# Expert weights in 2 MB slots of one piece, with the last expert's rows turned before the down product of the one before

## The chip, the cores and the metric

One core of a Trainium2 chip runs the kernel; the other cores are idle. The metric is the device time of one execution in microseconds (us). The engines' names here: PE or TensorE multiplies matrices and transposes (its weight loads are listed as PEld), DVE or VectorE and ACT or ScalarE work element by element, POOL or GpSimd too and issues some DMAs, SP or SyncE issues the DMAs of the weights. MB in the profile's rates are 10^6 bytes; a slot of 1 MB or 2 MB has 2^20 or 2^21 bytes.

## The reference

Two mixing blocks of sequence length 256 and width 1024 are computed first; the change lies in the mixture of experts behind them. It has 32 experts of width 1024, four of them for each token, all in fp32:

```python
def run_block(args):
    toks, e = args
    xb = h_pad[toks]
    gu = xb @ w_gu[e] + b_gu[e]
    g, u = gu[:, :D_EXPERT], gu[:, D_EXPERT:]
    g = jnp.minimum(g, SWIGLU_LIMIT)
    u = jnp.clip(u, -SWIGLU_LIMIT, SWIGLU_LIMIT)
    act = (u + 1.0) * (g * jax.nn.sigmoid(SWIGLU_ALPHA * g))
    return act @ w_dn[e] + b_dn[e]
```

The rows are weighted with the router's gates and summed for each token, and x + g_f times that sum is the output. h is modulated before: a normalised x times (1 + sc_f) plus sh_f.

## The kernel before

The two blocks run in the first 660 us or so; what follows is a loop over the 32 experts. Each expert has room for 64 of the 256 tokens (CAP); a loop over all experts for fuller ones stands behind a branch that this input doesn't take.

**The work of one expert.** For four experts at a time (GE) the rows are gathered: `gather` multiplies xh and xl (the two parts of the split x, tokens on the partitions) by the one-hot S, for each of 8 pieces k of 128 columns four matmuls of 256 columns, and `modulated` writes the piece of xg with a scale and a bias from mcol (k odd on ACT, L1280, k even on DVE, L1282). `up_proj` multiplies xg by w_gu into two PSUM tiles, G and U: for each k two halves hf of 512 columns for G and two for U, each with 64 of TensorE's columns, so that the two halves of a pair take their places side by side (L1310). `act` makes u from G and U on DVE and ACT (L1319 to L1325). `down_proj` turns u with four transposes T (L1334), ScalarE copies them to aT (L1336), and 32 matmuls make Y from aT and w_dn (L1344); a bias product stands ahead (L1339). DVE scales Y to y (L1347). `rows_T` transposes the gates GS to gst (L1298), and `combine` adds gst by y to four PSUM tiles acc (L1354).

**Weights.** `Ring` (L1181 to L1209) holds tiles e that SyncE fills in the order of their use: 8 slots for k of 1 MB (EARLY) that are loaded while the second block still runs, 10 more (LATE) and one on the tile h once they come free. A slot takes 128 rows of w_gu, 2048 values a row, or 256 rows of w_dn, two rows on a partition; it has 8 KB a partition. Slots 7 and 8 of LATE are two half tiles each (HALVES), with a DMA apiece. An expert needs 8 slots for up and 4 for down. A load waits until the products of the slot's last user are done.

**Order.** The loop for expert e writes: act, rows_T, up product k = 0 of e + 1, down product, combine, gathers for the next group (3, 3 and 2 of the k for the first three experts of a group), up product k = 1 to 7 of e + 1. For e = 30, up product k = 1 to 7 of expert 31 stands ahead of the down product. A scheduler orders each engine's instructions by what is ready, so what the code writes in one place can fill waits in another.

**Split weights.** In the blocks before the experts, `wchunk` splits each weight tile w into wh and wl (L200 and L201), from a rotation of NSPLIT = 6 each.

## Time and profile before

| what | value |
|---|---|
| runs | 1614.72, 1626.3, 1627.21 us; median 1626.3 |
| profiled execution | 1623.24 us |
| its span | 1621.5 us |
| granted clock of TensorE, mean | 0.983 |
| busy: PE | 1500.5 us, 93% |
| busy: PEld | 795.1 us, 49% |
| busy: DVE | 618.2 us, 38% |
| busy: ACT | 418.6 us, 26% |
| busy: POOL | 145.7 us, 9% |
| DMA | 518.96 MB, mean 320 GB/s |

The profile is of one execution. PE's rows count two records for each fp32 matmul; the order below counts one. The busy time of PE covers stages with different limits, and in the chain that ended last PE has 83%, DVE 9%, ACT 4%. "Idle before" is the time in which the engine stood still just ahead of a row, with what ended it behind the arrow.

### The profile page before, as it was taken

What the parts mean: (1) busy time and instruction counts of PE and PEld (TensorE: products, weight loads), DVE (VectorE), ACT (ScalarE), POOL (GpSimd) and SP (SyncE); (2) the same over time, 40 slices, a digit from 0 to 9 for tenths busy, and PEclk for the clock granted to TensorE, in tenths of its full rate; (3) what the DMA queues carried; (4) which work ended last, traced back from release to release, by engine and by line L of the source; (5) the groups of instructions that cost most, each with busy time, mean ns of one, the idle gap of its engine ahead of it and who ended that gap; (6) DMA issues with size and microseconds to landing.
All of it is one profiled execution on the core that took longest, in us unless ns stands there. A gap on an engine that the chain in (4) does not pass through costs nothing.

```text
span 1621.5 us, 19463 instructions
## 1 busy us (share of the span) xinstructions
PE 1500.5 (93%) x7533; PEld 795.1 (49%) x7533; DVE 618.2 (38%) x1337; ACT 418.6 (26%) x823; POOL 145.7 (9%) x210
## 2 busy tenths in 40 slices
PE   7999999998999999999899889889998998998997
PEld 5776778677767787533333333333333333333332
DVE  7666855687787875311111111111111111111111
ACT  4455455554566564200000000000000000000000
POOL 6640100010000000100000000000000000000000
PEclk9999999999999999999999999999999999999998
DMA  9464664464554358899999999999999999999993
GB/s 336 155 222 146 186 216 145 168 221 154 176 171 149 129 191 350 325 419 418 420 419 418 419 418 418 419 419 419 418 419 419 419 419 419 419 419 418 419 418 150
DMA packets 119316, 518.96 MB, mean 320 GB/s; under 512 B 13222, under 2 KB 22690, under 8 KB 75188
## 3 DMA queue, kind: packets, MB, share of 16 engines
q1 hardware_dynamic: 114288, 507.42, 79.8%
...
q8 instruction: 61, 1.00, 0.2%
...
q14 instruction: 35, 0.29, 0.0%
...
## 4 chain that ended last, share of the span: by engine, by line
PE 83%; DVE 9%; ACT 4%; issue 2%; DMA 1%; ACTq 0%; POOL 0%; SPq 0%; DVEq 0%
PE Y L1344 15%; PE G L1310 13%; PE U L1310 12%; PE pj L216 5%; PE pj L218 5%; PE pj L217 5%; PE acc L1354 4%; PE pj L235 2%; PE pj L236 2%; PE pm L1290 2%; PE pj L237 2%; PE T L1334 1%; PE pj L395 1%; DVE u L1325 1%; PE pj L226 1%
## 5 line engine op out<-in xcount | busy, mean ns | idle before, releaser
L1310 PE MATMUL G<-e,xg 128*64 128x512 f32 x1024 | 293.4, 596 | 2.2 <-DVE xg L1282 1.3
L1310 PE MATMUL U<-e,xg 128*64 128x512 f32 x1024 | 291.4, 594 | 0.0
L1344 PE MATMUL Y<-e,aT 128*64 128x512 f32 x1024 | 245.4, 620 | 1.7 <-ACT aT L1336 1.7
L116 DVE TENSOR_TENSOR wl<-w,wh 128x1024 fp32r<-128x1024 f32 (+2 forms) x155 | 185.9, 1209 | 66.8 <-ACT wh L115 65.7
L1321 ACT ACTIVATE s<-g 128x512 f32<-128x512 f32 x32 | 20.2, 630 | 653.3 <-DVE g L1319 653.3
L115 ACT CAST wh<-w 128x1024 fp32r<-128x1024 f32 (+2 forms) x155 | 156.2, 1013 | 85.4 <-PE pj L218 47.2
L1319 DVE TENSOR_SCALAR g<-G 128x512 f32<-128x512 f32 x32 | 22.1, 691 | 349.4 <-PE G L1314 349.4
L1310 PEld LDWEIGHTS U<-e,xg 128*64 128x64 f32 x1024 | 82.7, 137 | 145.5 <-issue 144.2
L1310 PEld LDWEIGHTS G<-e,xg 128*64 128x64 f32 x1024 | 79.6, 137 | 140.5 <-issue 129.7
L216 PE MATMUL pj<-wh,hTh 128*128 128x512 f32 (+4 forms) x352 | 131.0, 373 | 1.2 <-ACT hTh L115 1.0
L1344 PEld LDWEIGHTS Y<-e,aT 128*64 128x64 f32 x1024 | 69.2, 141 | 125.0 <-issue 114.8
L218 PE MATMUL pj<-wh,hTl 128*128 128x512 f32 (+4 forms) x352 | 129.0, 367 | 0.9 <-DVE hTl L116 0.9
L217 PE MATMUL pj<-wl,hTh 128*128 128x512 f32 (+4 forms) x352 | 129.3, 367 | 0.0
L1272 POOL TENSOR_SCALAR GS<-cst,posm,gate 128x128 f32<-128x128 f32 x64 | 51.1, 807 | 805.2 <-PE gst L1298 805.1
L1347 DVE TENSOR_TENSOR y<-Y,gfb 128x512 f32<-128x512 f32 x32 | 22.1, 691 | 232.3 <-PE Y L1344 232.3
L235 PE MATMUL pj<-hTh,wh 128*128 128x256 f32 x320 | 93.7, 293 | 0.2 <-DVE acc L926 0.2
L236 PE MATMUL pj<-hTl,wh 128*128 128x256 f32 x320 | 92.4, 289 | 0.0
L237 PE MATMUL pj<-hTh,wl 128*128 128x256 f32 x320 | 91.6, 288 | 0.1
L1354 PE MATMUL acc<-y,gst 64*128 64x512 f32 x256 | 63.6, 615 | 20.8 <-DVE y L1347 20.6
L216 PEld LDWEIGHTS pj<-wh,hTh 128*128 128x128 f32 x352 | 68.3, 194 | 19.5 <-issue 4.6
L218 PEld LDWEIGHTS pj<-wh,hTl 128*128 128x128 f32 x352 | 68.5, 195 | 12.9 <-DVE hTl L116 2.0
L217 PEld LDWEIGHTS pj<-wl,hTh 128*128 128x128 f32 x352 | 68.8, 196 | 9.6 <-issue 0.9
...
## 6 DMA issues: line engine op xcount, KB each, us to landing
e<-in_w_gu_dram SPq DMA_DIRECT2D x229, 1024.0 KB, 17.4
e<-in_w_dn_dram SPq DMA_DIRECT2D x115, 1024.0 KB, 17.4
...
```

The lines of the kernel that those rows point to most:

```text
L115: nc.scalar.copy(hi, src)
L116: nc.vector.tensor_sub(lo, src, hi.bitcast(F32))
L216: mm(ps[t][:, :n], X.hi[:, k, ts], wh[:, a:a + n], start=(k == 0), stop=False)
L217: mm(ps[t][:, :n], X.hi[:, k, ts], wl[:, a:a + n], start=False, stop=False)
L218: mm(ps[t][:, :n], X.lo[:, k, ts], wh[:, a:a + n], start=False, stop=(k == nk - 1))
L235: mm(p, wh[:, a:a + 128], X.hi[:, k], start=(k == 0), stop=False)
L236: mm(p, wh[:, a:a + 128], X.lo[:, k], start=False, stop=False)
L237: mm(p, wl[:, a:a + 128], X.hi[:, k], start=False, stop=(k == nk - 1))
L1272: nc.gpsimd.tensor_scalar(GS[:, t], slots[:, None, :].to_broadcast([128, 2, CAP]), posm[:, t, e:e + 1], gate[:, t, e:e + 1], op0=OP.is_equ ...
L1310: mm(P[64 * hf:64 * hf + 64, :], xk(k), w(c), start=(k == 0), stop=False)
L1344: mm(Y[64 * hf:64 * hf + 64, :], aT[:, 2 * (i % 2) + j, i // 2, :], w(D * j + 512 * hf), start=False, stop=(i == 3 and j == 1))
L1354: mm(acc[t][hf], gst[hs, t * 128:(t + 1) * 128], y[hs, :], start=False, stop=stop, **kw)
```

## The change

The ring's slots have 2 MB, 16 KB a partition in one piece, with one DMA each: 4 in EARLY and 5 in LATE, 18 MB in place of 19, without half tiles and without the slot on h. An up slot takes 256 rows of w_gu, with rows 2p and 2p + 1 on partition p, so a slot serves k = 0 and 1 (then 2 and 3, and so on); a down slot takes 512 rows of w_dn, four on a partition. An expert needs 4 slots for up and 2 for down. To match, `gather` reads xh and xl with a stride of two values, scale and bias of `modulated` come from a second tile mpair that is made like mcol (two DMAs on POOL's queue, two transposes, a copy), and T reads u with a stride of four values, where it was two.

`wh` and `wl` get explicit tags, so that the six pairs lie pair by pair. `act`, `turned` (the transposes and the copy) and `down_proj` are now three functions. For e = 30 the order is: T and aT of expert 30, up product k = 1 to 7 of expert 31, act and T of expert 31 (with s and aT in a free xg tile, `spare`), and then the down product of expert 30; for e = 31 only rows_T, the down product and combine are left.

The order of TensorE's instructions at two places, and SyncE's. First TensorE in the third expert of a group, from the second bias product of Y to gst. Before:

```order
L1339 MATMUL Y<-biases,selb 64x512
L1290 MATMUL pm<-S,xh 128x256
L1291 MATMUL pm<-S,xl 128x256
L1344 MATMUL Y<-e,aT 64x512 x4
L1290 MATMUL pm<-S,xh 128x256
L1291 MATMUL pm<-S,xl 128x256
L1290 MATMUL pm<-S,xh 128x256
L1291 MATMUL pm<-S,xl 128x256
L1290 MATMUL pm<-S,xh 128x256
L1291 MATMUL pm<-S,xl 128x256
L1344 MATMUL Y<-e,aT 64x512 x4
L1298 MATMUL gst<-cst,GS 128x128 x2
```

Now, from the same place:

```order
L1324 MATMUL G<-e,xg 64x512
L1302 MATMUL pm<-S,xh 128x256
L1302 MATMUL pm<-S,xl 128x256
L1302 MATMUL pm<-S,xh 128x256
L1302 MATMUL pm<-S,xl 128x256
L1324 MATMUL G<-e,xg 64x512
L1324 MATMUL U<-e,xg 64x512
L1302 MATMUL pm<-S,xh 128x256
L1302 MATMUL pm<-S,xl 128x256
L1302 MATMUL pm<-S,xh 128x256
L1302 MATMUL pm<-S,xl 128x256
L1324 MATMUL U<-e,xg 64x512
```

G and U here are halves of the pairs for k = 1 of the next expert. Behind the last row stand gst and then all 16 products of Y in one row: Y went from three pieces with gathers between them to the end, and one pair of G and one of U came in halves between the gathers.

The experts that gather nothing have the two whole pairs of k = 1 between the bias products and gst. At the end of the program, TensorE before, from down product 30 on:

```order
L1344 MATMUL Y<-e,aT 64x512 x16
L1354 MATMUL acc<-y,gst 128x512 x4
L1334 MATMUL T<-cst,u 128x128 x4
L1339 LDWEIGHTS selb
L1339 MATMUL Y<-biases,selb 64x512
L1339 LDWEIGHTS selb
L1339 MATMUL Y<-biases,selb 64x512
L1344 MATMUL Y<-e,aT 64x512 x16
L1354 MATMUL acc<-y,gst 128x512 x4
```

Now, from T of expert 31 on:

```order
L1349 MATMUL T<-cst,u 128x128 x4
L1359 LDWEIGHTS selb
L1359 MATMUL Y<-biases,selb 64x512
L1359 LDWEIGHTS selb
L1359 MATMUL Y<-biases,selb 64x512
L1364 MATMUL Y<-e,aT 64x512 x8
L1310 MATMUL gst<-cst,GS 128x128 x2
L1359 LDWEIGHTS selb
L1359 MATMUL Y<-biases,selb 64x512
L1359 LDWEIGHTS selb
L1359 MATMUL Y<-biases,selb 64x512
L1364 MATMUL Y<-e,aT 64x512 x8
```

T of expert 31 moved ahead of down product 30, gst with it into the middle of that product; behind the last row stand acc, the 16 products of Y for expert 31 and the last acc.

SyncE's loads of the ring, from the first on. Before:

```order
L1202 DMA e<-in_w_gu_dram 128x2048 x9
L1202 DMA e<-in_w_dn_dram 128x2048 x4
L1202 DMA e<-in_w_gu_dram 128x1024 x2
L1202 DMA e<-in_w_gu_dram 128x2048 x2
L1202 DMA e<-in_w_gu_dram 128x1024 x2
```

Now:

```order
L1218 DMA e<-in_w_gu_dram 128x4096 x5
L1218 DMA e<-in_w_dn_dram 128x4096 x2
L1218 DMA e<-in_w_gu_dram 128x4096 x4
L1218 DMA e<-in_w_dn_dram 128x4096 x2
L1218 DMA e<-in_w_gu_dram 128x4096 x4
```

The sizes are partitions by values. Where a slot of two half tiles comes round, two loads of 1024 values stood; now all loads have 4096.

The diff:

```diff
@@ -30,12 +30,11 @@
 GONE = -3.0e38
 LOW = -87.0
 SLOT = 1024
-ESLOT = 2048
+ESLOT = 4096
 NRAW = 8
 NSPLIT = 6
-EARLY = (7, 2, 3, 4, 5, 6, 1, 0)
-LATE = (3, 0, 1, 2, 4, 7, 5, 6, 8, 9)
-HALVES = {7: (0, 2), 8: (1, 3)}
+EARLY = (1, 2, 3, 0)
+LATE = (0, 1, 2, 3, 4)
 
 
 def host_constants():
@@ -122,6 +121,15 @@
     pa = pa_ctx.enter_context(pool("pa", 2, "right"))
     wsp = pa_ctx.enter_context(pool("wsp", NSPLIT, "right"))
     wp = pa_ctx.enter_context(pool("wp", NRAW, "right"))
+    nsplit = [1]
+
+    def half_of(j, i):
+        return wsp.tile([128, SLOT], F32R, tag=f"w{'hl'[j]}{i}", name=f"w{'hl'[j]}", bufs=1)
+
+
+    for i in range(NSPLIT):
+        for j in range(2):
+            half_of(j, i)
 
     first_ctx = ExitStack()
     a1 = first_ctx.enter_context(pool("a1", 1))
@@ -197,8 +205,8 @@
         got = []
         for k in range(0, nk, per):
             v = wload(src, off + k * 128 * stride, stride, per, cw, spare and k + per == nk)
-            hi = wsp.tile([128, SLOT], F32R, tag="wh", name="wh")[:, :per * cw]
-            lo = wsp.tile([128, SLOT], F32R, tag="wl", name="wl")[:, :per * cw]
+            hi, lo = (half_of(j, nsplit[0] % NSPLIT)[:, :per * cw] for j in range(2))
+            nsplit[0] += 1
             split(hi, lo, flat(v))
             for i in range(per):
                 got.append((hi[:, i * cw:(i + 1) * cw], lo[:, i * cw:(i + 1) * cw]))
@@ -356,6 +364,7 @@
     bfor = const.tile([128, 8], F32, name="bfor")
     nc.gpsimd.dma_start(bfor, bcast_rows(I["b_forget"], 0, 8))
     mcol = const.tile([128, 16], F32, name="mcol")
+    mpair = const.tile([128, 16], F32, name="mpair")
     lg0 = const.tile([128, NE], F32, name="lg0")
     wrt = const.tile([128, 8, NE], F32, name="wrt")
     nc.gpsimd.dma_start(wrt, dview(I["w_router_2"], 0, [[NE, 128], [128 * NE, 8], [1, NE]]))
@@ -1058,6 +1067,15 @@
             p = pm()
             nc.tensor.transpose(p[:, :16], mrow, ident[:16, :16])
             nc.vector.tensor_copy(mcol, p[:, :16])
+
+            mrow = aw.tile([128, 256], F32, tag="sco", name="mrow")[:8]
+            for i, v in enumerate((4, 3)):
+                nc.gpsimd.dma_start(mrow[4 * i:4 * i + 4], dview(mod, v * D, [[256, 4], [1, 256]]))
+            p = pm()
+            m2 = mrow.rearrange("p (f b) -> p b f", b=2)
+            for b in range(2):
+                nc.tensor.transpose(p[:, 8 * b:8 * b + 8], m2[:, b], ident[:8, :8])
+            nc.vector.tensor_copy(mpair.rearrange("p (q b) -> p b q", b=2), p[:, :16].rearrange("p (b q) -> p b q", b=2))
             p = pm()
             for k in range(8):
                 mm(p[:, :NE], mcol[:, 8 + k:9 + k].to_broadcast([128, 128]), wrt[:, k], start=(k == 0), stop=(k == 7))
@@ -1196,17 +1214,15 @@
             if ws is None:
                 ws = make(i)
             slot[2] = None
-            m = ESLOT // len(ws)
             rows = src[ds(e, 1), r0:r0 + 128 * (ESLOT // n)].rearrange("a (p k) c -> p (a k c)", p=128)
-            for j, w in enumerate(ws):
-                nc.sync.dma_start(w, rows[:, j * m:(j + 1) * m])
-            return lambda o: ws[o // m][:, o % m:o % m + 512]
+            nc.sync.dma_start(ws, rows)
+            return lambda o: ws[:, o:o + 512]
 
         def up(self, e, k):
-            return self.load(wgu, e, 128 * k, 2 * D)
+            return self.load(wgu, e, 256 * k, 2 * D)
 
         def down(self, e, i):
-            return self.load(wdn, e, 256 * i, D)
+            return self.load(wdn, e, 512 * i, D)
 
     def moe(ring, ap, mask, gate, posm, rr, xl, acc, place, gates_of):
         x = h
@@ -1215,15 +1231,11 @@
             late = es.enter_context(pool("late", 1, "right"))
 
             def late_slot(i):
-                if i not in HALVES:
-                    return [late.tile([128, ESLOT], F32, tag=f"e{i}", name="e")]
-                return [late.tile([128, ESLOT // 2], F32, tag=f"h{j}", name="e") for j in HALVES[i]]
-
-
-            for i in range(min(HALVES)):
+                return late.tile([128, ESLOT], F32, tag=f"e{i}", name="e")
+
+
+            for i in range(len(LATE)):
                 late_slot(i)
-            for j in range(2 * len(HALVES)):
-                late.tile([128, ESLOT // 2], F32, tag=f"h{j}", name="e")
             biases = aw.tile([96, 7, 512], BF, name="biases")[:, :6]
             nc.gpsimd.dma_start(biases, bscr)
             gfb = aw.tile([128, 512], F32, name="gfb")
@@ -1254,7 +1266,6 @@
             for t in range(2):
                 gates_of(t)
             ring.add(late_slot, LATE)
-            ring.add(lambda i: [res.tile([128, ESLOT], F32, tag="h", name="e")], (0,))
 
             def one_hot(e0, S=None):
 
@@ -1277,18 +1288,19 @@
             def modulated(o, p, k):
 
                 if k % 2:
-                    nc.scalar.activation(o, p, AF.Identity, bias=mcol[:, 8 + k:9 + k], scale=mcol[:, k:k + 1])
+                    nc.scalar.activation(o, p, AF.Identity, bias=mpair[:, 8 + k:9 + k], scale=mpair[:, k:k + 1])
                 else:
-                    nc.vector.tensor_scalar(o, p, mcol[:, k:k + 1], mcol[:, 8 + k:9 + k], op0=OP.mult, op1=OP.add)
+                    nc.vector.tensor_scalar(o, p, mpair[:, k:k + 1], mpair[:, 8 + k:9 + k], op0=OP.mult, op1=OP.add)
 
             def gather(S, xg, ks):
 
                 n = xg.shape[-1]
                 for k in ks:
-                    p, c = pm(), slice(k * 128, (k + 1) * 128)
+                    p = pm()
                     for t in range(2):
-                        mm(p[:, :n], xh[t][:, c], S[t], start=(t == 0), stop=False)
-                        mm(p[:, :n], xl[:, t, c], S[t], start=False, stop=(t == 1))
+                        for j, y in enumerate((xh[t], xl[:, t])):
+                            mm(p[:, :n], y.rearrange("p (a f b) -> p a b f", a=4, b=2)[:, k // 2, k % 2], S[t],
+                               start=(t == 0 and j == 0), stop=(t == 1 and j == 1))
                     modulated(xg[:, k], p[:, :n], k)
 
             def rows_T(GS):
@@ -1303,21 +1315,24 @@
             def up_proj(G, U, e, xk, sel, ks):
 
                 for k in ks:
-                    w = ring.ahead.pop(0) if ring.ahead else ring.up(e, k)
+                    if k % 2 == 0:
+                        ring.now = ring.ahead.pop(0) if ring.ahead else ring.up(e, k // 2)
+                    w = ring.now
                     for b, P in enumerate((G, U)):
                         for hf in range(2):
-                            c = 1024 * b + 512 * hf
+                            c = 2048 * (k % 2) + 1024 * b + 512 * hf
                             mm(P[64 * hf:64 * hf + 64, :], xk(k), w(c), start=(k == 0), stop=False)
                     if k == 7:
                         for b, P in enumerate((G, U)):
                             for hf in range(2):
                                 mm(P[64 * hf:64 * hf + 64, :], sel, biases[:, 2 * b + hf], start=False, stop=True)
 
-            def act(G, U):
+            def act(G, U, s=None):
 
                 g = pb.tile([128, 512], F32, tag="u", name="g")
                 nc.vector.tensor_scalar(g, G, 7.0, None, op0=OP.min)
-                s = aw.tile([128, 512], F32, tag="s", name="s")
+                if s is None:
+                    s = aw.tile([128, 512], F32, tag="s", name="s")
                 nc.scalar.activation(s, g, AF.Sigmoid, scale=1.702)
                 u = pb.tile([128, 512], F32, tag="u", name="u")
                 nc.vector.tensor_scalar(u, U, 7.0, -7.0, op0=OP.min, op1=OP.max)
@@ -1325,24 +1340,29 @@
                 nc.vector.scalar_tensor_tensor(u, u, 1.0, g, op0=OP.add, op1=OP.mult)
                 return u
 
-            def down_proj(e, u, sel):
+            def turned(u, aT=None):
 
                 T = pm("T")
 
-                u4 = u.rearrange("p (a f b) -> p a b f", a=2, b=2)
+                u4 = u.rearrange("p (f b) -> p b f", b=4)
                 for j in range(4):
-                    nc.tensor.transpose(T[:, j * 128:(j + 1) * 128], u4[:, j // 2, j % 2], ident)
-                aT = aw.tile([128, 512], F32, tag="s", name="aT").rearrange("p (j h s) -> p j h s", j=4, h=2)
-                nc.scalar.copy(aT, T.rearrange("p (j h s) -> p j h s", j=4, h=2))
+                    nc.tensor.transpose(T[:, j * 128:(j + 1) * 128], u4[:, j], ident)
+                if aT is None:
+                    aT = aw.tile([128, 512], F32, tag="s", name="aT")
+                nc.scalar.copy(aT, T)
+                return aT.rearrange("p (j h s) -> p j h s", j=4, h=2)
+
+            def down_proj(e, aT, sel):
+
                 Y = pm("Y")
                 for hf in range(2):
                     mm(Y[64 * hf:64 * hf + 64, :], sel, biases[:, 4 + hf], start=True, stop=False)
-                for i in range(4):
+                for i in range(2):
                     w = ring.down(e, i)
-                    for j in range(2):
+                    for j in range(4):
                         for hf in range(2):
-                            mm(Y[64 * hf:64 * hf + 64, :], aT[:, 2 * (i % 2) + j, i // 2, :],
-                               w(D * j + 512 * hf), start=False, stop=(i == 3 and j == 1))
+                            mm(Y[64 * hf:64 * hf + 64, :], aT[:, j, i, :], w(D * j + 512 * hf), start=False,
+                               stop=(i == 1 and j == 3))
                 y = pb.tile([128, 512], F32, tag="u", name="y")
                 nc.vector.tensor_mul(y, Y, gfb)
                 return y
@@ -1371,16 +1391,24 @@
                 el = e % GE
                 if el == 0 and e:
                     xg = nxg
+                if e + 1 == NE:
+                    combine(rows_T(GS), down_proj(e, last, chosen(e)), True)
+                    break
                 u = act(*P)
                 gst = rows_T(GS)
                 if e + 1 < NE:
                     GS = gated(e + 1)
                     P = pm("G"), pm("U")
                     start(e + 1, nxg if el == GE - 1 else xg, range(1), P)
+                aT = turned(u)
                 if e + 2 == NE:
+
                     start(e + 1, xg, range(1, 8), P)
-                y = down_proj(e, u, chosen(e))
-                combine(gst, y, e == NE - 1)
+                    spare = flat(aw.tile([128, 8, GE * CAP], F32, tag="xg", name="spare", bufs=2))
+                    u = act(*P, s=spare[:, :512])
+                    last = turned(u, spare[:, 512:1024])
+                y = down_proj(e, aT, chosen(e))
+                combine(gst, y, False)
                 if el == 0 and e + GE < NE:
                     nS, nxg = one_hot(e + GE)
                 if e == NE // 4:
@@ -1429,7 +1457,7 @@
                         P = pm("G"), pm("U")
                         sel = se.to_broadcast([96, 64])
                         up_proj(*P, ev, lambda k: xg[:, k], sel, range(8))
-                        y = down_proj(ev, act(*P), sel)
+                        y = down_proj(ev, turned(act(*P)), sel)
                         combine(gst, y, True, skip_group_check=True)
                 store()
 
@@ -1440,7 +1468,7 @@
     with pool("ring", 1) as rp, pool("b", 1) as ap:
         ring = Ring()
         xl = rp.tile([128, 2, D], F32R, name="xl")
-        ring.add(lambda i: [rp.tile([128, ESLOT], F32, tag=f"e{i}", name="e")], EARLY)
+        ring.add(lambda i: rp.tile([128, ESLOT], F32, tag=f"e{i}", name="e"), EARLY)
         routed = mix_out(ring, ap, xl)
         pa_ctx.close()
         moe(ring, ap, *routed)
```

## Rows read from the trace of the kernel before

**Rows 1.** Stretches: length, busy time (instructions) by engine, PEclk, DMA share, GB/s.

```profile
620.00:630.00 10.00, 10.00 (x49) 8.19 (x48) 5.67 (x6) 5.66 (x7) 0.00 (x0) 1.00 1.02 425
667.00:671.00 4.00, 4.00 (x16) 1.91 (x12) 0.00 (x0) 0.38 (x1) 2.60 (x4) 0.57 1.04 375
724.50:1560.00 835.50, 758.51 (x3488) 268.78 (x3486) 125.78 (x209) 49.23 (x83) 44.29 (x56) 0.99 1.01 419
1590.00:1600.00 10.00, 7.95 (x36) 2.42 (x32) 3.19 (x6) 0.63 (x1) 0.00 (x0) 1.00 0.31 127
1600.00:1610.00 10.00, 9.11 (x36) 3.26 (x38) 0.41 (x1) 0.58 (x1) 0.00 (x0) 0.83 0.00 0
```


**Rows 2.** TensorE's groups, 664 to 1612: busy us, mean ns, idle before, releasers.

```profile
L1310 PE MATMUL G<-e,xg 128*64 128x512 f32 x1024 | 293.4, 596 | 2.2 <-DVE xg L1282 1.3 <-ACT xg L1280 0.8
...
L1344 PE MATMUL Y<-e,aT 128*64 128x512 f32 x1024 | 245.4, 620 | 1.7 <-ACT aT L1336 1.7
L1354 PE MATMUL acc<-y,gst 64*128 64x512 f32 x250 | 62.3, 616 | 20.8 <-DVE y L1347 20.6
L1290 PE MATMUL pm<-S,xh 128*128 128x256 f32 x127 | 41.6, 346 | 17.5 <-DVE xg L1282 7.0 <-ACT aT L1336 5.1 <-ACT xg L1280 4.6
...
L1334 PE MATMUL T<-cst,u 128*128 128x128 f32 x128 | 23.0, 302 | 33.6 <-DVE u L1325 33.6
...
L1298 PE MATMUL gst<-cst,GS 128*128 128x128 f32 x64 | 13.8, 299 | 10.2 <-ACT aT L1336 4.3 <-ACT xg L1280 3.7 <-DVE xg L1282 2.2
```


**Rows 3.** SyncE's queue: waited for: us in total, times, longest us.

```profile
SPq L1202 <- PE U L1310: 129.1, 90, 6.2
...
SPq L1202 <- PE Y L1344: 76.3, 50, 5.8
```


**Rows 4.** Timeline of TensorE, the last experts: start, us, instruction, idle before.

```profile
1574.60 0.71 PE L1334 MATMUL T<-cst,u 128*128 128x128 f32 x4 [1.12 <-DVE u L1325]
...
1576.42 1.08 PE L1310 MATMUL G<-e,xg 128*64 128x512 f32 x4
1577.33 1.03 PE L1310 MATMUL U<-e,xg 128*64 128x512 f32 x4
...
1588.49 0.39 PE L1314 MATMUL G<-biases,selb 96*64 96x512 bf16 x2
...
1588.92 7.04 PE L1344 MATMUL Y<-e,aT 128*64 128x512 f32 x32
...
1600.56 0.72 PE L1334 MATMUL T<-cst,u 128*128 128x128 f32 x4 [1.81 <-DVE u L1325]
...
1601.95 8.79 PE L1344 MATMUL Y<-e,aT 128*64 128x512 f32 x32 [0.34 <-ACT aT L1336]
1611.53 1.99 PE L1354 MATMUL acc<-y,gst 64*128 64x512 f32 x8 [0.79 <-DVE y L1347]
```


**Rows 5.** Timeline of TensorE, gather products without a gap, third expert of a group.

```profile
1109.73 0.29 PE L1290 MATMUL pm<-S,xh 128*128 128x256 f32 x1
1109.85 0.28 PE L1291 MATMUL pm<-S,xl 128*128 128x256 f32 x1
```


**Rows 6.** Timeline of TensorE, one half of G alone, ahead of acc.

```profile
1262.40 1.02 PE L1310 MATMUL G<-e,xg 128*64 128x512 f32 x2
1263.36 1.99 PE L1354 MATMUL acc<-y,gst 64*128 64x512 f32 x8
```


**Rows 7.** Timeline of TensorE, transposes of a contiguous operand in the second block.

```profile
645.97 0.63 PE L1122 MATMUL pm<-cst,h 128*128 128x128 f32 x4
```


**Rows 8.** Timeline of VectorE, where act of expert 30 begins.

```profile
1571.59 0.69 DVE L1319 TENSOR_SCALAR g<-G 128x512 f32<-128x512 f32 x1 [11.95 <-PE G L1314]
```


**Rows 9.** DMA issues: times, KB each, median us from issue to landing.

```profile
e<-in_w_gu_dram SPq DMA_DIRECT2D x229, 1024.0 KB, 17.4
```


**Rows 10.** TensorE's weight loads, 664 to 1612: busy us, mean ns, idle before.

```profile
L1334 PEld LDWEIGHTS T<-cst,u 128*128 128x128 f32 x128 | 17.8, 208 | 60.8 <-issue 52.6 <-PE U L1310 8.2
```

## The prediction

> **What bounds the kernel now.** I read the stage windows first, to find the stage that is worth anything, then the groups of TensorE's lines in the expert stage, then what SyncE's queue waits for, and last the timelines of single experts.
>
> The experts take the span from about 664 us to its end. In the long middle window [rows 1] TensorE is busy 758.51 of 835.5 us at a granted clock of 0.99, while the DMA engines are busy 1.01 of the time at 419 GB/s: two resources are nearly full at once, and the reader has to see which of them ends later. The groups of TensorE [rows 2] answer that. G (up product) idled 2.2 us and Y (down product) 1.7 us in the whole stage, both for results of VectorE or ScalarE; no group names a weight transfer. What TensorE does wait for are its own dependent steps: T for u 33.6 us, acc for y 20.8, pm (gather) for xg and aT 17.5, gst for aT and xg 10.2. So the chain of dependent steps on TensorE sets the end. SyncE's queue says the same from the other side: 140 of its issues waited 205.4 us for U and Y to give a slot back [rows 3], so the loads were often ahead and wanted room. But the stream is right behind: it runs at its full 419 GB/s until 1590, the 10 us after that move 127 GB/s, that is 1.27 MB or 3 us at the full rate, and then nothing [rows 1]. I put its end at D = 1593. The last acc starts at 1611.53 [rows 4], 18.5 us later. That margin limits every gain on TensorE in this stage.
>
> The profiled execution took 1623.24 us, 3.1 less than the median of 1626.3 (runs 1614.72 to 1627.21). The sums below are made against 1623.24.
>
> **The change part by part.** *Stalls covered.* A 2 MB up slot holds k = 0 and k = 1, so up(e+1, 1) is at hand when up(e+1, 0) is, and the new order of TensorE puts it between the T transposes, the gathers and gst. Removed waits: for aT 5.1 + 4.3 + 1.7 = 11.1 us, for xg in the gathers 7.0 + 4.6 = 11.6, for xg before gst 3.7 + 2.2 = 5.9 [rows 2]. A stall costs more than its gap: in a run without gaps a matmul of the gather starts 0.12 us after the one before although that one lasts 0.29 [rows 5], so 0.17 of overlap goes with each. Counted in the timeline of the stage these are 31 stalls for aT, 18 for xg in the gathers and 8 for xg before gst, a mean of 0.36 for aT and 0.64 for xg, so 57 x 0.17 = 9.7 more. Sum -38.3 us. What covers each is a product of 0.86 us; without that cover all of it stays. The waits of T for u and of acc for y get no filler in the new order and stay.
>
> *Pairs torn apart.* G's two halves of 64 columns normally run side by side: the 14 pairs of up(31) between 1576.42 and the biases at 1588.49 take 0.86 us each [rows 4]. In the new order the pair G and the pair U of k = 1 stand as half, gather, half + half, gather, half. A half alone costs as much as a pair: at 1262.40 one half of G takes 1.02 us and acc starts 0.96 after it [rows 6]. Three slots of 0.86 instead of two, in the 21 experts that gather for the next group (3 in each of 7 groups): 21 x 0.86 = +18.1. Bounds: 0, if a lone half runs beside the gather, and twice that, if the halves in the middle do not run side by side. I take +18.1, as the row is the same operation. Two more changes between kinds of product in each of these experts cost 0.05 each (the first G after gst lasts 1.08, the U behind it 1.03 [rows 4]): 42 x 0.05 = +2.1.
>
> *Strided reads.* T's stationary is u with a stride of 4 values where it was 2, and the gathers read xh and xl with stride 2 where they were contiguous. Stride 2 is priced by two rows: four transposes of a contiguous h take 0.63 us [rows 7], four of u with stride 2 take 0.71 [rows 4], that is 0.02 each. 128 T and 224 gather products at 0.02: +7.0. Bounds: 0, if the wider stride costs no more than stride 2 and the loads hide, and +26.6 for T if a load doubles (rival E).
>
> [...]
>
> *The end.* The act and T of expert 31 come ahead of down product 30. Before, T(31) waited 1.81 and Y(31) ran 1.75 slow [rows 4]; with overlap 3.7 (the waits for aT are in the sum above). After, act(31) starts when up(31) ends, TensorE has T(31) next and nothing else: from g at 1571.59 [rows 8] to T at 1574.60 [rows 4] is 3.0, with overlap 3.2. Net -0.5. Bounds: -3.7, if Y(30) were put ahead of T(31), which the order doesn't do, and +1.2, if the clock drops there as it did before.
>
> *Slots and ring.* 18 MB in place of 19: 1 MB less lead is 2.5 us at 419 GB/s, out of 18.5 at the end. Weight tiles wh and wl lie elsewhere with the same six in rotation; I cost it at nothing, since each split waits for the tile six before it as it did. mpair adds two small transposes and a copy before the stage: by T's mean of 0.30 [rows 2] below 1 us, I take +0.5.
>
> TensorE's sum: -38.3 + 18.1 + 2.1 + 7.0 - 3.7 - 0.5 + 0.5 = -14.8; acc(31) would start at 1596.7.
>
> *The stream's own limit.* From 724.5 to D = 1593 at 419 GB/s 364 MB flow. No row has a packet of 16 KB a partition. Nearest: the 10 us in which the ring's first loads, of 8 KB a partition, come in moved 425 GB/s [rows 1]; 1 MB loads take 17.4 us from issue to landing [rows 9], which is 7.3 MB in flight at that rate, so more in flight has little to give. Bounds 419 (D = 1593) and 425 (D = 1581); I take 422 (D = 1587), the middle. The four down slots, 8.4 MB or 19.9 us, are the last to come, so the last slot of up(31) lands at D - 19.9. From there: four pairs 3.4, biases 0.4, act 3.2, T 0.7, which is D - 12.2; Y(30) 6.9 and gst 0.4, D - 4.9; y 0.9 and acc(30) 1.9, D - 2.1; Y(31) 6.9, D + 4.8; y 0.9, so acc(31) starts at D + 5.8 (durations from [rows 4], less what overlaps). That is 1599 at 419 and 1593 at 422. TensorE's own 1596.7 is the later one of the middle values by 4: the two limits nearly coincide, and a much larger gain on TensorE would not show.
>
> [...]
>
> **The rivals.**
> A, forecast: both limits as above, 1600 to 1612 us; middle 1623.24 - 14.8 = 1608.
>
> B, torn pairs and strides eat the gain: if the middle halves do not run side by side (+18) or strides cost twice (+7) the sum is between -8 and +3: 1615 to 1627. For it: the gaps were 0.36 and 0.64 and a filler takes 0.86, so the torn pair eats most of what one expert gains. Against: the order puts G's second half and U's first next to each other.
>
> C, all favourable: strides free, the clock drops gone, stream at 425: TensorE -14.8 - 7.0 - 3.7 = -25.5, the stream 1581 + 5.8 = 1587, that is -24.7. Time 1599. For it: weight loads lie beside products; against: T's own stall of 1.12 [rows 4], ahead of the clock drops, stays.
>
> D, other side: pieces of 16 KB a partition stream slower, since one queue entry holds its engine longer, or fewer loads are ready at a time. TensorE has no lead to give: From D = 1605.7 on, at 364 MB / 881.2 us = 413 GB/s, acc(31) is later than the old 1611.5. 1% slower needs D = 1622, 406 GB/s; at 400 D is 1634.5 and the time 1652. For it: the ring of 9 slots frees room in steps of 2 MB, and SyncE's issues wait for U and Y [rows 3]; against: with 8 KB a partition the DMA engines are busy all of the time [rows 1], so what counts is only how they fare with longer pieces, and nothing in those rows speaks of a loss there.
>
> E, wide stride: T reads one value of each 16 bytes. T's loads take 208 ns each [rows 10]; doubled and unhidden, 128 x 0.208 = +26.6 in place of T's 2.6: sum +9.2, time 1632, no change that can be told. [...]
>
> **How the numbers follow.** A 0.40, B 0.25, C 0.12, D 0.11, E 0.07, and 0.05 for less gain than B of another cause. The predicted time is A's middle, 1608, which is 1.1% under the median 1626.3. About 1% is what can be told from no change: faster is below 1610, slower above 1642. A lies below 1610 with some three quarters of its chance (0.31), C wholly: 0.43 faster. D is slower from 406 GB/s down, most of its chance, and E if its loads take more than double: 0.10. The rest, 0.47, is the same. The range 1595 to 1632 holds A, B, C, E and the near end of D; A's own is 1600 to 1612.
>
> **What would show it.** Right: no idle before pm and gst for aT and xg; k = 1 halves of G and U between gathers at three times 0.86 us; T groups of four at about 0.79; DMA share 1.01 with 419 to 425 GB/s and D near 1587; acc(31) near 1597. Wrong: TensorE idle for e (weights) in G or Y, which is D; T at 1.5 us, E; a middle pair at 1.7 us, B; clock drops as many as before, then +3.7.

## The result, and the profile after

The changed kernel takes 1605.37 us (median of 4 runs, 1597.59 to 1609.67) against 1626.76 us; the ratio is 0.9876 with a 95% interval of 0.9843 to 0.9909, a gain of 1.2% that the interval keeps clear of 1. The forecast was 1608 us, in a range of 1595 to 1632, with 0.43 for faster and 0.47 for no change. In a later set of runs the same kernel had 1602.93 us and 0.9871 (0.9834 to 0.9908).

The profiled execution took 1605.46 us, its span 1603.7. These are the lines that answer to those of before. First the windows of the expert stage (columns as in [rows 1]):

```profile
724.50:1560.00 835.50, 780.60 (x3588) 276.54 (x3586) 128.81 (x214) 51.08 (x86) 44.48 (x56) 1.00 1.01 427
...
1580.00:1590.00 10.00, 9.20 (x44) 2.95 (x42) 1.12 (x2) 0.00 (x0) 0.00 (x0) 1.00 0.28 120
```

TensorE is busy 780.60 us of the long window where it was 758.51, at a granted clock of 1.00, and the weights flow at 427 GB/s in place of 419. After 1580 there are 1.2 MB left, 2.8 us at that rate, but the rate falls off at the end: the last load lands at 1587.4, and before it landed at 1596.4. Counted from the first acc of each profile (below) that is 15.4 us earlier, 877.8 for 893.2. TensorE's groups from 664 to 1600 us (columns as in [rows 2]):

```profile
L1324 PE MATMUL G<-e,xg 128*64 128x512 f32 x1024 | 295.1, 597 | 2.1 <-ACT xg L1291 1.0 <-DVE xg L1293 0.9 <-DMA e<-in_w_gu_dram 0.2
L1364 PE MATMUL Y<-e,aT 128*64 128x512 f32 x992 | 223.5, 598 | 0.0
L1374 PE MATMUL acc<-y,gst 64*128 64x512 f32 x256 | 63.6, 615 | 23.8 <-DVE y L1367 23.8
L1302 PE MATMUL pm<-S,xh 128*128 128x256 f32 x128 | 40.5, 338 | 0.8 <-DVE S L1247 0.8
...
L1349 PE MATMUL T<-cst,u 128*128 128x128 f32 x128 | 23.4, 306 | 34.7 <-DVE u L1340 34.7
L1310 PE MATMUL gst<-cst,GS 128*128 128x128 f32 x64 | 13.9, 299 | 0.7 <-DVE xg L1293 0.7
```

The waits that the change was to cover are gone: pm fell from 17.5 to 0.8 us, gst from 10.2 to 0.7, Y from 1.7 to 0. The waits of T for u (33.6, now 34.7) and of acc for y (20.8, now 23.8) stay, as forecast. There is one new releaser, a weight transfer, with 0.2 us at G. Where it stands, the timeline of the last experts shows (start, duration, instruction, idle before it):

```profile
1567.90 1.08 PE L1324 MATMUL G<-e,xg 128*64 128x512 f32 x4 [0.18 <-DMA e<-in_w_gu_dram]
...
1574.76 1.10 PE L1349 MATMUL T<-cst,u 128*128 128x128 f32 x4 [2.77 <-DVE u L1340]
...
1576.22 4.42 PE L1364 MATMUL Y<-e,aT 128*64 128x512 f32 x16
...
1581.19 3.60 PE L1364 MATMUL Y<-e,aT 128*64 128x512 f32 x16
...
1587.50 7.09 PE L1364 MATMUL Y<-e,spare 128*64 128x512 f32 x32
1595.38 1.99 PE L1374 MATMUL acc<-y,gst 64*128 64x512 f32 x8 [0.79 <-DVE y L1367]
```

The last slot of up(31) arrives at 1567.9, TensorE had been ready 0.18 us earlier. From there on T(31) waits 2.77 for its act, as worked out, the granted clock drops to 0.51 (1574.4 to 1577.8 us; T 1.10 for 0.72, Y's first half 4.42 for 3.60), and the last acc starts at 1595.38, where the forecast had 1596.7. The chain that ended last says the same in one line (start, duration, piece):

```profile
1534.42 33.44 DMA e<-in_w_gu_dram
```

Before, no transfer of expert weights stood there; now the chain runs through one. SyncE's queue (us in total, times, longest) and the issue row (times, KB, us to landing) show that the loads mostly waited for a slot to come free:

```profile
SPq L1218 <- PE U L1324: 406.2, 78, 14.7
...
SPq L1218 <- PE Y L1364: 167.9, 49, 5.8
```

```profile
e<-in_w_gu_dram SPq DMA_DIRECT2D x128, 2048.0 KB, 18.7
```

The first acc of the stage starts at 709.59 us and the last at 1595.38: 885.8 us. Before it was 703.18 to 1611.53 [rows 4], 908.4 us. This stretch has the same work in every kernel here, and the blocks ahead of it, where the granted clock stood at 0.50 for 31 us in the profile of before and for 41 us in this one, lie outside. I use it below as "the stage": the change shortened it by 22.6 us. The 6.4 us by which the first acc came later in this one profile and the 1.6 by which its end came sooner behind the last acc make up the rest of the 17.8 us between the two spans.

### The profile page after: what moved, and what is told of

It reads as the page before. It is cut to its first block, busy times and chain, and to the rows that moved or that the text cites. A ratio compares the mean times of both kernels' runs of the same rounds, so it can differ in the third digit from the quotient of the medians.

```text
span 1603.7 us, 19009 instructions
## 1 busy us (share of the span) xinstructions
PE 1507.3 (94%) x7535; PEld 799.8 (50%) x7535; DVE 615.9 (38%) x1338; ACT 418.7 (26%) x823; POOL 146.2 (9%) x212
## 4 chain that ended last, share of the span: by engine, by line
PE 83%; DVE 8%; DMA 4%; ACT 3%; issue 1%; ACTq 0%; DVEq 0%; SPq 0%
PE Y L1364 14%; PE G L1324 13%; PE U L1324 12%; PE pj L224 5%; PE pj L226 5%; PE pj L225 5%; PE acc L1374 4%; PE pm L1302 3%; PE pj L243 2%; DMA e<-in_w_gu_dram 2%; PE pj L244 2%; PE pj L245 2%; PE T L1349 1%; PE pj L404 1%; DMA w<-in_w_in_dram 1%
## 5 line engine op out<-in xcount | busy, mean ns | idle before, releaser
L1324 PE MATMUL G<-e,xg 128*64 128x512 f32 x1024 | 295.1, 597 | 2.1 <-ACT xg L1291 1.0
L1324 PE MATMUL U<-e,xg 128*64 128x512 f32 x1024 | 295.2, 596 | 0.0
L1364 PE MATMUL Y<-e,aT 128*64 128x512 f32 x992 | 223.5, 598 | 0.0
L1324 PEld LDWEIGHTS U<-e,xg 128*64 128x64 f32 x1024 | 78.3, 137 | 138.1 <-issue 134.8
L1324 PEld LDWEIGHTS G<-e,xg 128*64 128x64 f32 x1024 | 76.2, 136 | 127.1 <-issue 113.0
L1374 PE MATMUL acc<-y,gst 64*128 64x512 f32 x256 | 63.6, 615 | 23.8 <-DVE y L1367 23.8
```

Source lines behind the costliest of these rows:

```text
L1324: mm(P[64 * hf:64 * hf + 64, :], xk(k), w(c), start=(k == 0), stop=False)
L1364: mm(Y[64 * hf:64 * hf + 64, :], aT[:, j, i, :], w(D * j + 512 * hf), start=False, stop=(i == 1 and j == 3))
L1374: mm(acc[t][hf], gst[hs, t * 128:(t + 1) * 128], y[hs, :], start=False, stop=stop, **kw)
```

## The experiments

Two theories were to be told apart. S, the forecast's: TensorE's own chain became shorter by the fill of its waits, and the stream of weights ends almost together with it, so both limit. T: TensorE's order alone sets the time. Later two more on single parts: F, that the filler is what helps TensorE, and R, that the faster stream alone is.

| kernel | median us | ratio to before | 95% interval | first acc | stage us |
|---|---|---|---|---|---|
| before | 1622.65 to 1626.76 | 1 | | 703.18 | 908.4 |
| changed | 1605.37 | 0.9876 | 0.9843 to 0.9909 | 709.59 | 885.8 |
| e_two | 1623.99 | 0.9991 | 0.9963 to 1.0018 | 708.05 | 908.0 |
| e_light | 1595.09 | 0.9820 | 0.9765 to 0.9876 | 702.18 | 878.9 |
| e_tfirst | 1600.24 | 0.9834 | 0.9783 to 0.9886 | 708.77 | 886.8 |
| e_tfirst_light | 1569.17 | 0.9660 | 0.9608 to 0.9711 | 699.55 | 857.5 |
| e_8k | 1613.51 | 0.9932 | 0.9909 to 0.9955 | 708.90 | 897.9 |
| e_nofill | 1642.09 | 1.0111 | 1.0074 to 1.0149 | 703.13 | 936.3 |
| e_oldsplit | 1607.18 | 0.9891 | 0.9856 to 0.9925 | 701.56 | 890.4 |
| e_newtail | 1596.73 | 0.9828 | 0.9793 to 0.9864 | 700.90 | 882.1 |
| e_after_b | 1602.93 | 0.9871 | 0.9834 to 0.9908 | 701.26 | 886.9 |
| e_newtail_b | 1596.67 | 0.9842 | 0.9802 to 0.9882 | 699.57 | 881.4 |
| e_best | 1598.22 | 0.9843 | 0.9804 to 0.9882 | 702.96 | 882.5 |

### Less for TensorE to do: e_tfirst, and the same with less to load: e_tfirst_light

The products k = 1 go whole between k = 0 and T (the later calls of start begin at k = 2), and pin keeps the first transpose behind what stands ahead of it on TensorE:

```diff
-                    start(e + 1, nxg if el == GE - 1 else xg, range(1), P)
+                    start(e + 1, nxg if el == GE - 1 else xg, range(2), P)
...
-                    nc.tensor.transpose(T[:, j * 128:(j + 1) * 128], u4[:, j], ident)
+                    tr = nc.tensor.transpose(T[:, j * 128:(j + 1) * 128], u4[:, j], ident)
+                    if j == 0:
+                        pin(tr)
```

e_tfirst_light also uses the first down slot twice:

```diff
+                w = ring.down(e, 0)
                 for i in range(2):
-                    w = ring.down(e, i)
```

> The changed kernel with the products k = 1 of the next expert put whole between k = 0 and T, so that T's wait for u is covered and no pair is torn, while the waits for aT and xg come back. On TensorE: -34.7 - 5 (T's waits with overlap) - 18 (torn pairs), + 16 (aT) + 20 (xg): about -20 us. Theory S: nearly none of it shows, since the weights come no earlier: 1600 to 1607 us, and G or Y now wait for weights. Rival T: all of it shows, 1583 to 1590 us.

> e_tfirst and e_light together (the output is not the reference's): k = 1 whole ahead of T, and one of two down slots loaded. Theories S and T alike: the stream no longer limits, so the -20 us of TensorE show, 1580 to 1590 us. If it stays above 1597 us, the order of e_tfirst gains less on TensorE than worked out, and e_tfirst says nothing about the stream.

With all weights to load nothing of TensorE's gain is in the stage, 886.8 us against 885.8. With a sixth fewer it is 857.5, where e_light (below), which also has a sixth fewer, has 878.9. The time of e_tfirst_light, 1569.17 us, lies 11 below its range of 1580 to 1590: with fewer loads the scheduler wrote another order in more places than the edit, as e_light shows. TensorE's groups in e_tfirst, 664 to 1620 us:

```profile
L1324 PE MATMUL G<-e,xg 128*64 128x512 f32 x1024 | 275.2, 597 | 13.7 <-DMA e<-in_w_gu_dram 12.1 <-ACT xg L1291 1.0 <-DVE xg L1293 0.7
...
L1366 PE MATMUL Y<-e,aT 128*64 128x512 f32 x992 | 228.6, 606 | 2.2 <-DMA e<-in_w_dn_dram 1.8 <-ACT aT L1354 0.3
...
L1302 PE MATMUL pm<-S,xh 128*128 128x256 f32 x128 | 40.2, 336 | 20.1 <-DVE xg L1293 8.3 <-ACT aT L1354 6.1 <-ACT xg L1291 4.6
...
L1349 PE MATMUL T<-cst,u 128*128 128x128 f32 x128 | 24.2, 313 | 2.8 <-DVE u L1340 2.8
```

T's wait fell from 34.7 to 2.8 us, pm's rose from 0.8 to 20.1 as the filler left it, and what was won is lost in a new place: G waits 12.1 and Y 1.8 us for weights. The timeline of its end:

```profile
1566.64 1.08 PE L1324 MATMUL G<-e,xg 128*64 128x512 f32 x4 [1.25 <-DMA e<-in_w_gu_dram]
...
1595.58 1.99 PE L1376 MATMUL acc<-y,gst 64*128 64x512 f32 x8 [0.80 <-DVE y L1369]
```

The last acc starts at 1595.58, in the changed kernel at 1595.38, although TensorE was 11.3 us ahead of the changed kernel by the 23rd acc, counted from the first. In e_tfirst_light the same line of G has no such wait:

```profile
L1324 PE MATMUL G<-e,xg 128*64 128x512 f32 x1024 | 388.7, 597 | 1.6 <-ACT xg L1291 1.0 <-DVE xg L1293 0.7
```

S holds: in the changed kernel the stream and TensorE's own chain come to the last up slot within 0.2 us of each other, and what a faster TensorE gains ahead of that slot it waits for weights. (e_tfirst's median is 5 us under the changed kernel's, and 2.7 under that of its later runs, but the intervals overlap and the profiles have the same end.)

### Less to load: e_light

The second edit above, alone, in the changed kernel.

> The changed kernel with only the first of the two down slots of each expert loaded and used twice (a sixth of the expert weights is not read, so the output is not the reference's); all products stay. The stream has then room. Theory S: TensorE's own chain is only just ahead of the stream's limit, so at most 4 us faster than the changed kernel: 1601 to 1606 us, with no wait for weights. Rival L (the stream holds TensorE back over the whole stage): more than 8 us faster, under 1597 us.

The time, 1595.09 us, lies on rival L's side, but the run cannot tell S from L, for TensorE's order is another in every expert of the stage. Its groups, 664 to 1650 us:

```profile
L1324 PE MATMUL G<-e,xg 128*64 128x512 f32 x1024 | 413.9, 597 | 1.8 <-DVE xg L1293 1.0 <-ACT xg L1291 0.8
...
L1374 PE MATMUL acc<-y,gst 64*128 64x512 f32 x256 | 63.6, 615 | 1.0 <-DVE y L1367 1.0
```

A half of G now stands ahead of acc and covers its wait for y (1.0 us in place of 23.8), and most pairs of G and U are torn for it (413.9 us busy in place of 295.1). From the ninth period from acc to acc on the two come out even: a group of four experts takes 115.8 us in e_light and 115.8 in the changed kernel. The stage is 6.9 us shorter because of the first eight periods (5.4) and because the granted clock stays at 1.00 in the tail (1.8). That the stream does not hold TensorE over the changed kernel's long middle is not shown by this run; it is read from the changed kernel's own rows, where G waits 0.2 us for weights and Y not at all.

### The same slots with pieces of 8 KB: e_two and e_8k

e_two fills each slot with two loads:

```diff
-            nc.sync.dma_start(ws, rows)
+            for j in range(2):
+                nc.sync.dma_start(ws[:, j * 2048:(j + 1) * 2048], rows[:, j * 2048:(j + 1) * 2048])
```

> The changed kernel with each 2 MB slot filled by two loads of 1 MB (8 KB a partition each) in place of one with 16 KB a partition; slots, order and arithmetic as in the changed kernel. Theory S (stream and TensorE's own chain now end together, and the stream sets the end from the last up slot on): the rate falls from 427 back to about 419 GB/s, the weights that flow after 724 us (some 364 MB) take 364 x (1/0.419 - 1/0.427) = 16 us longer, and the time rises by 10 to 16 us, to 1615 to 1621 us. Rival T (TensorE's chain alone sets the end, the rate has room): within 3 us of the changed kernel, 1602 to 1609 us.

All of the gain is gone: 1623.99 us, 3 above the range of S, and a stage of 908.0. But not for the reason of S. The groups of TensorE, 664 to 1620 us:

```profile
L1325 PE MATMUL G<-e,xg 128*64 128x512 f32 x1024 | 300.6, 607 | 1.6 <-ACT xg L1292 1.0 <-DVE xg L1294 0.7
...
L1303 PE MATMUL pm<-S,xh 128*128 128x256 f32 x128 | 41.7, 346 | 7.2 <-ACT aT L1353 5.8 <-DVE S L1248 0.8 <-DVE xg L1294 0.6
...
L1311 PE MATMUL gst<-cst,GS 128*128 128x128 f32 x64 | 13.8, 297 | 5.4 <-ACT aT L1353 3.9 <-ACT xg L1292 0.7 <-DVE xg L1294 0.7
```

G waits for no weights; pm waits 5.8 us and gst 3.9 for aT again. In most experts k = 1 now stands behind the first products of the gather, or behind gst where nothing is gathered, so that it covers less while the pairs are still torn; the granted clock drops seven times in the stage, too (windows of 4 us at 0.57 to 0.74). (That the scheduler takes k = 1 as ready later when a slot has two loads is the likely reason; no run shows it apart.) The waits of pm and gst are 11.1 us longer than in the changed kernel, and six more drops at about 1.7 us (a set of Y takes 8.79 us in one and 7.04 outside [rows 4]) are 10, together 21 of the 22.2 us. The rate was 420 GB/s, the last load landed 16.7 us ahead of the last acc, and TensorE alone set the time. So this run mixes two things. It shows that one load for both k is part of what moved the order, and nothing on the rate.

e_8k changes the rate and, for TensorE, only the strides. One load per slot, in two pieces a partition whose rows are 128 (up) and 256 (down) apart; gather then reads xh and xl without a stride, and T reads u with stride 2:

```diff
-            rows = src[...].rearrange("a (p k) c -> p (a k c)", p=128)
-            nc.sync.dma_start(ws, rows)
+            rows = src[...].rearrange("a (h p k) c -> p (a h) (k c)", h=2, p=128)
+            nc.sync.dma_start(ws.rearrange("p (h x) -> p h x", h=2), rows)
...
-                u4 = u.rearrange("p (f b) -> p b f", b=4)
+                u4 = u.rearrange("p (a f b) -> p a b f", a=2, b=2)
```

> The changed kernel with one load per 2 MB slot still, but in two pieces of 8 KB a partition (rows 128 apart for up, 256 apart for down), so that xh, xl are read without a stride, u with a stride of 2 as before, with the scales from mcol; the order of TensorE's instructions is the same as in the changed kernel, row by row. Theory S (stream and TensorE end together in the changed kernel): the rate falls from 427 to about 420 GB/s, the last weights land about 12 us later (as they did in e_two), and with the order unchanged TensorE now waits for them: 1614 to 1620 us. Rival T (TensorE's order alone is the gain): 1602 to 1609 us. The stride terms show in the same run: T x4 at 0.71 in place of 0.72 and no change in the gathers would price the strides at nothing, in place of the 7.0 us of the forecast.

TensorE's order is the changed kernel's, instruction by instruction. The middle of the stage, then TensorE's groups:

```profile
724.50:1540.00 815.50, 758.00 (x3472) 266.44 (x3470) 124.77 (x207) 49.82 (x84) 44.29 (x56) 1.00 1.01 421
```

```profile
L1324 PE MATMUL G<-e,xg 128*64 128x512 f32 x1024 | 295.6, 598 | 14.7 <-DMA e<-in_w_gu_dram 12.9 <-ACT xg L1291 1.0 <-DVE xg L1293 0.8
...
L1364 PE MATMUL Y<-e,aT 128*64 128x512 f32 x992 | 223.4, 597 | 3.7 <-DMA e<-in_w_dn_dram 3.7
...
L1349 PE MATMUL T<-cst,u 128*128 128x128 f32 x128 | 23.2, 303 | 28.4 <-DVE u L1340 28.4
```

The rate is 421 GB/s, and TensorE now waits 12.9 us for up weights and 3.7 for down weights, nearly all of it from 1446 us on, in the last experts. Stage 897.9 us, 12.1 longer; the median 1613.51 us, 8 to 11 above the changed kernel's (1605.37 and 1602.93). That is 0.5 us under S's range and 4.5 over T's; the waits for weights are what S had named. So of the 20 us about half come only because the stream got faster. The same run prices the strides: T takes 303 ns with stride 2 and 306 with stride 4, and the 3 ns are the four transposes of expert 31 that the changed kernel runs at the lower clock (1.10 us for 0.72).

### Without the filler: e_nofill

The products k = 1 are held behind the last acc of the expert before them (start hands pin to each of them); the call for the fourth expert of a group gets pin, too:

```diff
...
                 combine(gst, y, False)
+                if e + 2 < NE and el < GE - 1:
+                    start(e + 1, nxg if el == GE - 1 else xg, range(1, 8), P, pin)
...
```

> The changed kernel with the products k = 1 of the next expert held behind the last acc of the expert before, so that they fill no wait and no pair is torn; 16 KB pieces, 427 GB/s and the tail of e = 30 as in the changed kernel. Theory F (the filler pays for the gain on TensorE): waits for aT and xg come back, the torn pairs go: +12 us from the order as the experts' periods show it (about 18 by the forecast's own terms), and up to 9 more if the clock drops come back with the waits: 1616 to 1627 us. Rival R (the rate alone): within 3 us of the changed kernel, 1602 to 1609 us.

1642.09 us: slower than the kernel before, and slower than F's range. TensorE's groups, 664 to 1650 us:

```profile
L1366 PE MATMUL Y<-e,aT 128*64 128x512 f32 x992 | 249.4, 655 | 0.7 <-ACT aT L1354 0.7
...
L1302 PE MATMUL pm<-S,xh 128*128 128x256 f32 x128 | 45.5, 373 | 26.6 <-DVE xg L1293 11.5 <-ACT xg L1291 7.9 <-ACT aT L1354 6.1
```

pm's waits are back with 26.6 us, and Y's mean is 655 ns where it was 598. That is the clock, as two windows and the timeline of an expert that gathers show:

```profile
724.50:1540.00 815.50, 732.53 (x3294) 264.58 (x3292) 118.11 (x197) 46.81 (x79) 43.11 (x54) 0.95 0.98 409
1462.00:1472.00 10.00, 9.31 (x32) 3.98 (x34) 0.54 (x1) 0.56 (x1) 0.90 (x2) 0.66 1.01 428
```

```profile
1459.25 0.72 PE L1351 MATMUL T<-cst,u 128*128 128x128 f32 x4 [1.12 <-DVE u L1342]
...
1460.64 0.40 PE L1302 MATMUL pm<-S,xh 128*128 128x256 f32 x1 [0.34 <-ACT aT L1354]
...
1462.05 0.48 PE L1302 MATMUL pm<-S,xh 128*128 128x256 f32 x1 [0.66 <-ACT xg L1291]
...
1463.82 0.58 PE L1302 MATMUL pm<-S,xh 128*128 128x256 f32 x1 [0.64 <-DVE xg L1293]
...
1464.97 5.66 PE L1366 MATMUL Y<-e,aT 128*64 128x512 f32 x16
...
1470.93 3.65 PE L1366 MATMUL Y<-e,aT 128*64 128x512 f32 x16
```

Three waits follow each other here (aT 0.34, xg 0.66, xg 0.64), behind T's 1.12, and the granted clock falls to 0.50 (1464 to 1468 us): the first 16 products of Y take 5.66 us, the second 3.65. The granted clock of the middle stretch is 0.95 where the changed kernel has 1.00. It drops 15 times in the stage, mostly in such an expert. In these runs the drops go with T's wait and others behind it together: e_tfirst has the waits behind T as well (pm 20.1 us), but not T's own, and its clock drops once ahead of its last experts (0.57 over 924 to 928 us); the changed kernel has T's wait without those behind it (pm 0.8 us), and its clock doesn't drop there at all (1.00 over 709.59 to 1570 us). F holds and R is refuted: with the fast stream and without the filler the kernel is slower than before. What I had not reckoned with is the order itself: the kernel before had pieces of Y between its gathers, and e_nofill has the gathers in a row.

### Where the split tiles lie: e_oldsplit

wh and wl as in the kernel before:

```diff
-            hi, lo = (half_of(j, nsplit[0] % NSPLIT)[:, :per * cw] for j in range(2))
-            nsplit[0] += 1
+            hi = wsp.tile([128, SLOT], F32R, tag="wh", name="wh")[:, :per * cw]
+            lo = wsp.tile([128, SLOT], F32R, tag="wl", name="wl")[:, :per * cw]
```

> The changed kernel with wh and wl in the two rotations of six that they had before, not pair by pair. Theory: where the split tiles lie costs nothing; within 4 us of the changed kernel, 1601 to 1610 us, and the first acc at 700 to 710 us as elsewhere. Rival: the layout cost or gave the 6.4 us by which the changed kernel's profile reached its first acc later (709.59 against 703.18 us): 1596 to 1600 us, with the first acc near 703.

1607.18 us, inside the interval of the changed kernel. The first acc starts at 701.56, and at 701.26 in e_after_b, which is the changed kernel once more: the 6.4 us belong to the first profile's execution and not to the layout. Ahead of its first acc the granted clock stood at 0.50 for 41 us, in e_oldsplit for 27. But the layout is not free. With the same start the stage is 3.5 us longer than in e_after_b (890.4 for 886.9), and TensorE waits 4.8 us for weights in the last experts, where e_after_b waits for none. The loads of the ring show where it comes from (650 to 660 us, e_oldsplit, then e_after_b; the last two columns are DMA share and GB/s):

```profile
650.00:660.00 10.00, 9.98 (x53) 7.34 (x52) 6.02 (x20) 4.11 (x10) 0.25 (x1) 1.00 0.49 184
```

```profile
650.00:660.00 10.00, 9.98 (x53) 7.38 (x52) 6.03 (x20) 4.28 (x10) 0.26 (x1) 1.00 1.02 434
```

With the old layout SyncE sends the seventh load at 658.1 us, after 13.9 us of waiting for a product of the block ahead (pj); in e_after_b the seventh goes at 644.5. So in the old layout that slot's place is free later. Counted from the first acc, the last load lands at 882.1 us where it lands at 877.3 in e_after_b, and these 4.8 us are what TensorE waits. In the median of the time this doesn't show beyond the noise.

### A shorter tail: e_newtail, and with e_tfirst: e_best

T of expert 31 behind down product 30 (the scheduler puts it behind its first half), act still ahead:

```diff
                     u = act(*P, s=spare[:, :512])
+                y = down_proj(e, aT, chosen(e))
+                if e + 2 == NE:
                     last = turned(u, spare[:, 512:1024])
-                y = down_proj(e, aT, chosen(e))
                 combine(gst, y, False)
```

> The changed kernel with T of expert 31 behind the first half of down product 30 in place of ahead of it; act(31) still ahead of it, so its 3 us lie beside the 16 products of Y. Theory: TensorE doesn't wait 2.77 us for u there, Y(30) starts when its weights are in, and the last acc starts 3 to 4 us earlier than the 52.8 us after acc 29 that the changed kernel has (that is 49 to 50), with the clock drop at 1574 gone too: 1600 to 1603 us. Rival: the last down weights land at their old time and hold Y(31), no change in those 52.8 us.

The timeline of its last experts:

```profile
1563.94 3.65 PE L1364 MATMUL Y<-e,aT 128*64 128x512 f32 x16 [0.84 <-DMA e<-in_w_dn_dram]
1567.53 0.75 PE L1349 MATMUL T<-cst,u 128*128 128x128 f32 x4
...
1568.74 3.65 PE L1364 MATMUL Y<-e,aT 128*64 128x512 f32 x16
...
1582.98 1.99 PE L1374 MATMUL acc<-y,gst 64*128 64x512 f32 x8 [0.79 <-DVE y L1367]
```

Y(30) starts 0.84 us after TensorE is ready, when its weights are in, and T(31) follows the first half without a wait. From acc 29 to the last acc it takes 49.1 us, against 52.8 (53.9 in e_after_b): 3.7 to 4.8 less, as expected. The median of 1596.73 us is 8.6 under the changed kernel's and 3 under the expected range, lower than that gives, so it ran again beside the changed kernel:

> The changed kernel once more, beside the next two on the same chip: 1600 to 1610 us, ratio to before 0.985 to 0.991. The last acc 8 us after the last weight landed; the first acc anywhere from 700 to 710 us by how often the clock dropped in the blocks ahead of the experts.

> e_newtail once more: by its profile the stretch from acc 29 to the last acc is 3.7 us shorter than in the changed kernel, so 2 to 6 us faster than e_after_b. If the 8.6 us between the medians of the earlier calls were the tail's, 7 to 10 us faster.

> e_tfirst and e_newtail together. Theory S: the stream sets the end in both, so the 25 us that TensorE gains by e_tfirst in the long run do not show, and only the shorter tail does: within 4 us of e_newtail_b, with TensorE waiting for weights 10 to 20 us. Rival T: 15 to 25 us faster than e_newtail_b.

Medians 1602.93, 1596.67 and 1598.22 us; stages 886.9, 881.4 and 882.5. The shorter tail gives 5.5 us of stage, within the expected 2 to 6, and 6.3 of the median; some 2 to 3 of the 8.6 were the chance of one set of runs. The intervals of the ratios overlap, so that e_newtail is the better kernel by about 5 us rests on the stages of two profiles each. e_best has TensorE waiting 12.9 and 3.9 us for weights and gains nothing over it, as S says.

## Why the prediction was right

**The outcome and the main reading.** The sum gave 1608 us and the two limits were said to coincide nearly, so that a larger gain on TensorE would not show. e_tfirst is that larger gain, and it doesn't show; e_8k is the slower stream, and it does. That TensorE and not the stream set the kernel before was read rightly from [rows 2, 3]: its groups had no wait for weights.

**The terms**, as the runs have them:

| term | forecast | measured |
|---|---|---|
| waits for aT and xg covered | -38.3 | -27.9 us of gaps in the groups, of 28.6 counted; their overlap (9.7 in the forecast) was not measured apart |
| torn pairs and changes of kind | +20.2 | +25.8 |
| strided reads | +7.0 | 0 |
| clock drops | -3.7 | -8.5 |
| end of the stage | -0.5 | -1.5 (acc 29 to the last acc: 54.35 us before, 52.83 now) |
| stage in all | -15.3 (without mpair) | -22.6 |

With the overlap as forecast these sum to -21.8. The torn pairs were mis-sized by more than a quarter. The timeline of a gathering expert in the changed kernel shows the three slots:

```profile
1218.29 1.02 PE L1324 MATMUL G<-e,xg 128*64 128x512 f32 x2
1219.24 0.40 PE L1302 MATMUL pm<-S,xh 128*128 128x256 f32 x1
...
1219.60 0.28 PE L1302 MATMUL pm<-S,xh 128*128 128x256 f32 x1
1219.71 0.28 PE L1302 MATMUL pm<-S,xl 128*128 128x256 f32 x1
1219.93 0.64 PE L1324 MATMUL G<-e,xg 128*64 128x512 f32 x1
...
1220.93 0.39 PE L1302 MATMUL pm<-S,xh 128*128 128x256 f32 x1
...
1221.62 1.07 PE L1324 MATMUL U<-e,xg 128*64 128x512 f32 x2
1222.62 0.44 PE L1310 MATMUL gst<-cst,GS 128*128 128x128 f32 x2
```

G's half takes 0.95 us to the next start, the halves of G and U side by side 1.00, U's half 1.00: 2.95 where two whole pairs take 1.72, so 1.23 in each of 21 experts. The forecast had 0.96 of it (0.86 and two changes at 0.05); each of the three blocks takes 0.95 to 1.00, where it had reckoned with 0.86.

The strides were the term that failed. I took 0.02 us for each operand from four transposes of u against four of h [rows 4, 7], and put it down to the stride. e_8k shows T's mean 3 ns apart between stride 2 and 4, and the gathers go at a pitch of 0.11 to 0.12 us with a stride (1219.60 to 1219.71) and without one [rows 5]. The difference between those two rows must have another cause, which was not looked for. Rival E has no support: with one value in 16 bytes a transpose takes 306 ns, with two 303 (e_8k), and T's weight loads take 209 ns each where they took 208 [rows 10].

No run shows the -3.7 us that the sum has for the clock. What the traces show in its place: before, the granted clock stands at 0.50 for 3.4 us six times behind the first acc, each time behind a wait of T for u (1.11 us, the last 1.81) and one for aT (0.34 or 0.43); of these six drops five are gone and one is left, in the tail at 1574, at about 1.7 us each as in [rows 4], so -8.5. T's wait of 1.1 us is still in the experts, and up to 1570 us the granted clock stays at 1.00 with it. e_nofill is the counterpart: more waits behind it, and the clock falls in most gathering experts (15 drops).

**The stream.** 427 GB/s lies above my upper bound of 425, which was the rate of one stretch of 10 us [rows 1]. D came out at the forecast's 1587 by luck. At 427 the forecast's sum gives 724.5 + 364/0.427 = 1577, and acc(31) at 1583. But the last load of the kernel before landed at 1596.4, 3.4 us behind the 1593 that the amount alone gave, and in the changed kernel's profile the ring's first load went out at 620.8 us where it was 614.0, 6.8 later, with the blocks ahead of it; together that is 1587. The last slot of up(31) landed 1567.9; from there the forecast had 25.7 us to the last acc, the trace has 27.5, with 1.8 of it from the clock drop. The bound failed because I looked for rows with the same piece size, and none had the longer one. By an estimate from the two rates, 427 and 419 GB/s over 16 engines, a piece of 16 KB takes 614 ns and two of 8 KB take 626, 12 ns more; what these 12 ns are no run shows.

The layout of wh and wl was put at nothing. That holds for the blocks ahead, whose end it doesn't move (first acc at 701.56 and 701.26 us), but not for the ring: e_oldsplit lands its last load 4.8 us later, counted from the first acc, and TensorE waits as long for weights.

**The sum's luck.** Strides and clock were forecast too unfavourably, by 7.0 and 4.8, the torn pairs too favourably, by 5.6. They leave 6.2 of the 7.3 us by which the stage beat the sum; in the first profile the late first acc took them back. The median of 1605 is therefore a better match to 1608 than the terms earned.

**The other rivals.** D (a slower stream) fell with 427 GB/s. B had its condition half: torn pairs cost more, but strides nothing. C had its stream, its free strides and all but one of its missing clock drops; it was the nearest rival, and the 5.6 us that the torn pairs cost beyond the forecast lie between its 1599 us and the time.

Not settled is why four transposes of h took 0.08 us less than four of u.
